# A late-tile mask moved to VectorE, transposes of one bank kept together, and a new table of offsets

## The chip, the cores and the metric

The kernel runs on one core of one Trainium2 chip. The metric is the device time of one execution in microseconds (us). Durations in the text are us unless marked ns. TensorE is called PE in the profile, VectorE DVE, ScalarE ACT, GpSimd POOL, and SyncE, which issues the loads, SP.

## What is computed

One decoder layer on 512 tokens of width 1024: token mixing, cross-attention into 256 memory tokens, and a squared-ReLU MLP of width 4096. The part that the change touches is the attention inside token mixing: 8 query heads on 2 KV heads of 64 columns, with three branches (compressed, selected, window). With 512 tokens, 8 blocks of 64 and a top-k of 16, every block is selected, so the selected branch and the window branch are both causal attention over all earlier tokens, each with its own keys and values:

```python
s = jnp.einsum('bthgd,bhtmd->bhgtm', qc, kg) * scale
p = masked_softmax(s, mask)                  # mask: key position <= query position
o_slc = einsum(p, vg)                        # the window branch is the same with its own k, v
o = g[..., 0:1] * o_cmp + g[..., 1:2] * o_slc + g[..., 2:3] * o_win
```

`masked_softmax` puts minus infinity where the mask is false, subtracts the row's maximum, takes the exponential, and divides by the sum.

## The kernel before

The Python program lists all instructions and a planner, the class `Plan`, orders them. `add` (L204) takes down each instruction with its cost (`cost`, L140), its dependences and a rank. The rank is the instruction's place in the program, moved by a lead and by an entry of the table `LEADS` (L57), which is looked up by the name of the stage. `schedule` then runs a clock per engine: `choose` (L318) takes for each engine the instructions that could start first and among these the one with the highest rank; `start` (L304) says when that would be. The order that comes out is issued as it is, the DMAs on SP's queue among it, so each engine works through a fixed list, in order. All instructions therefore show one line of the source in the profile, L405.

Matrix products are done in three passes, since each operand is split into a high and a low part (`split`: ScalarE casts the high part, VectorE subtracts it to get the low one). One PSUM bank holds 128 x 512 floats, and there are 8 of them.

Attention goes over the query tiles t = 0 to 3 of 128 rows, over the KV heads and over pairs of query heads, so there are 16 units, each with two heads (e = 0, 1), in 32 steps. A step has these parts:

- `scores` (L964): two matmuls per branch, of the query tile with the high keys `KB` and the low keys `KL`, into a bank; n = 128 (t + 1) columns. Where both branches fit into one bank (t = 0, 1) they share it. For t = 2 and 3 (n = 384 and 512) each branch b has its own bank. Then a third matmul, bf16, of the identity `idb` with `tri` (0 on and under the diagonal, -1e38 above) adds the mask to the last 128 columns.
- `soft` (L985): VectorE takes the negated row maximum from the bank (TENSOR_REDUCE), ScalarE the exponential, from the bank to an SBUF tile `P` (6 buffers), with the row sum as a second output.
- `scale`: VectorE or GpSimd multiplies `P` by the reciprocal of the sum and the gate.
- `turn`: four transposes of 128 x 128 per bank bring the `P` tiles of the unit before to the layout that the product with the values needs; in the rows they are the matmuls `ps<-idf,P`. ScalarE and VectorE split them out of the bank.
- `values` and `evac`: the products with the values, among them four with the compressed branch's `Vc` that have only 128 moving columns (`ps<-pt,Vc`).

Work that doesn't depend on attention ("fill": the gating unit, memory keys and values) is placed between these steps. After it come the output projection and the cross-attention of each row tile (the `ch_` stages; `ch_v` has further matmuls of 128 columns, `ps<-b,b`), then the two halves of the MLP, ff1 and ff2. Other fp32 transposes, with moving operand 128 x 128, are in the profile as `ps<-idf,z`, `ps<-idf,b` and `ps<-idf,bT`.

Of the kernel before, what the change touches and what calls it, by code (L numbers as in the profile page):

```python
# [9 lines left out]
F32 = mybir.dt.float32  # L10
# [43 lines left out]
         "wa": dict(w=3, raw=2),  # L54
         "wf": dict(w=1, raw=1)}

LEADS = {"ch_f0": -1174, "ch_f1": -1572, "ch_f2": -903, "ch_norm1": 1885, "ch_norm2": 867, "ch_norm3": -7928,  # L57
# [21 lines left out]


class Plan:
# [15 lines left out]

    TABLES, TABLE = {AF.Exp: 0, AF.Tanh: 0, AF.Gelu_apprx_tanh: 1}, 1283

    SPARE = (0, 300, 0, 0, 0)  # L100

    def __init__(self, tc, share):
        self.tc, self.nc, self.share = tc, tc.nc, share
        self.ops, self.loads, self.lead, self.queue, self.stage, self.stages = [], [], 0.0, None, None, []
        self.home, self.last, self.reads, self.tables = {}, {}, {}, []
        self.tiles, self.uses, self.caps, self.index = [], [], {}, {}
        for e in self.ENGINES:
            setattr(self, e, self._Engine(self, e))
# [31 lines left out]
    def cost(self, eng, op, aps, func):  # L140
        n = max(self.width(a) for a, _ in aps)
        if eng == "tensor":
            if op == "transpose" and all(a.dtype == F32 for a, _ in aps):
                return 109
            return max(25, n / 2.4 + (15 if n > 200 else 7))
        if eng == "sync":
            run = min(list(a.ap)[-1][1] for a, _ in aps)
            return max(450, 4 * n * max(list(a.ap)[0][1] for a, _ in aps) / (230 if run <= 128 else 290))
        psum = any(bank for _, bank in aps)
        part = 100 if eng != "gpsimd" and min(list(a.ap)[0][1] for a, _ in aps) < P and n > 32 else 0  # L150
        if eng == "vector" and any(len(a.ap) > 2 and list(a.ap)[-1][0] > 4 for a, _ in aps):
            part = 0.9 * n
        scalars = sum(1 for a, _ in aps if self.width(a) == 1) if n > 1 else 0
        if eng == "scalar":
            return n / 1.2 + (52 if psum else 93) + 93 * scalars + part
        if eng == "vector":
            if op == "reciprocal":
                return 68 + 6.3 * n
            fast = op in ("tensor_scalar", "tensor_copy") and not psum
            return 68 + n / (1.92 if fast else 0.96) + 61 * (scalars > (op == "tensor_reduce")) + part  # L160
        if op in ("tensor_tensor", "square"):
            return 300 + 165 * n if func == OP.pow else 150 + 2.1 * n
        return 244 + 0.84 * n + 82 * (scalars > 1) if op == "tensor_scalar" else 130 + 0.9 * n
# [40 lines left out]
    def add(self, ways, args, kw):  # L204
# [50 lines left out]
                for e, op in ways]  # L255
        self.loads.append(self.load(ways[0][1], args[1]) if ways[0][0] == 0 else 0.0)
        self.tables.append(next((self.TABLES[a] for a in args if isinstance(a, AF) and a in self.TABLES), None))
        self.stages.append(self.stage)
        self.ops.append((ways, args, kw, sorted(deps), used, self.lead + LEADS.get(self.stage, 0) - i))

    def schedule(self):
# [12 lines left out]
        active, held, uses = set(), set(), [len(u) for u in self.uses]  # L274
        ends = [{} for _ in self.tiles]
        free, begun, table = [0.0] * ne, 0.0, 0

        port = {1: 0.0, 3: 0.0}
        known = [[-1e9] * ne for _ in ops]
# [22 lines left out]
            return max([0.0] + [t + lat[x][e] for x, t in f])  # L302

        def start(i, e):  # L304
            t = max(free[e], begun + self.loads[i]) if e == 0 else free[e]
            if e == 2 and self.tables[i] not in (None, table):
                t += self.TABLE
            if e in port and next(w for w in ops[i][0] if w[0] == e)[3]:
                t = max(t, port[4 - e])
            for x in range(ne):  # L310
                t = max(t, known[i][x] + lat[x][e])
            return t
# [5 lines left out]
        def choose(e):  # L318
# [15 lines left out]
            if not ts:  # L334
                return None
            lim = min(ts)[0]
            r, t, i = max((ops[i][5], t, i) for t, i in ts if t <= lim)
            return t, -r, i, e

# [4 lines left out]
        while len(out) < len(ops):  # L344
# [25 lines left out]
                stale[4 - e] = True  # L370
            if e == 0:
                begun = t
            if e == 2 and self.tables[i] is not None:
                table = self.tables[i]
            span = max(span, end)
# [33 lines left out]
def hybrid_block(ctx, tc, x, mem, norm_mix_g, w_in, sg_ln_g, sg_ln_b, sg_w, sg_b, q_norm_g,  # L409
# [346 lines left out]
    for t in range(TT):  # L756
# [9 lines left out]
    nc.stage = "masks"  # L766
    idb = cpool.tile([P, P], BF16, name="idb")
    dve.tensor_copy(idb, idf)
    tri = cpool.tile([P, P], BF16, name="tri")
    tri32 = ztile()[:, :P]  # L770
    pool.memset(tri32, 0.0)
    pool.affine_select(out=tri32, in_=tri32, pattern=[[-1, P]], compare_op=OP.is_ge,
                       fill=NEG, base=0, channel_multiplier=1)
    dve.tensor_copy(tri, tri32)
    cmk = cpool.tile([P, TT, 32], BF16, name="cmk")
# [176 lines left out]
    class Pair:  # L952
# [11 lines left out]
        def scores(self, e):  # L964
            kvh, n = self.kvh, self.n
            g = 2 * self.pr + e
            q = self.qT[:, g * P:g * P + P]
            if 2 * n <= 512:
                S = bank()[:, :2 * n].rearrange("p (b n) -> p b n", b=2)
                for i, k in enumerate((KB, KL)):  # L970
                    nc.tensor.matmul(S, q, k[:, kvh, :, :n], start=i == 0, stop=False)
                nc.tensor.matmul(S[:, :, n - P:n], idb, bc(tri[:, None, :], [P, 2, P]), start=False, stop=True)
                self.S[e] = [S]
            else:
                self.S[e] = []
                for b in range(2):
                    S = bank()[:, :n]
                    for i, k in enumerate((KB, KL)):
                        nc.tensor.matmul(S, q, k[:, kvh, b, :n], start=i == 0, stop=False)
                    nc.tensor.matmul(S[:, n - P:n], idb, tri, start=False, stop=True)  # L980
                    self.S[e].append(S)
            self.mx[e], self.den[e] = small(2), small(2)
            self.Ps[e] = []

        def soft(self, e, b):  # L985
            Ss, mx = self.S[e], self.mx[e]
            if len(Ss) == 2:
                dve.tensor_reduce(mx[:, b:b + 1], Ss[b], AX.X, OP.max, negate=True)
            elif b == 0:
                dve.tensor_reduce(mx, Ss[0], AX.X, OP.max, negate=True)  # L990
            S = Ss[b] if len(Ss) == 2 else Ss[0][:, b, :]
            self.Ps[e].append(zpool.tile([P, 512], F32, tag="P", bufs=6, name=nm("P"))[:, :self.n])
            act(self.Ps[e][b], S, AF.Exp, bias=mx[:, b:b + 1], accum_out=self.den[e][:, b:b + 1])

        def scale(self, e):
            h = self.kvh * G + 2 * self.pr + e
# [439 lines left out]
```

## Time and profile before

| | us |
|---|---|
| median of 3 runs | 701.18 (699.33 to 701.6) |
| profiled execution, its own time | 699.56 |
| its span, first to last instruction | 697.8 |
| PE busy | 689.5 (99%) |
| DVE busy | 415.2 (59%) |
| ACT busy | 318.2 (46%) |
| POOL busy | 79.2 (11%) |
| granted TensorE clock, mean of the core | 1.000 |

How to read it: busy time of PE is modelled, since matmuls are pipelined. In a timeline the start of a matmul plus its length is its end, and the difference of two ends that follow each other is what the second one cost. Rows of several equal matmuls carry a count (x4), and their length runs from the first start to the last end.

### The profile page before, as it was taken

To read this page: it belongs to the slowest core of one execution; us is meant where nothing else is said; L and a number is where in the kernel's file an instruction comes from. 1 tells how busy PE (TensorE), PEld (TensorE's weight loads), DVE (VectorE), ACT (ScalarE), POOL (GpSimd) and SP (SyncE) were. 2 spreads that over 40 slices of the span, in tenths; PEclk is the share of its full clock that TensorE was granted. 3 is DMA by queue.
4 is the path that set the end of the run, shared out by engine and by line. 5 is a ranking of instruction groups with operands and counts; after the bars stand their busy time and mean duration, and the time that the engine had idled before them with its cause. 6 is when DMAs were issued, how large, how long until landed. Compare 5 with 4: busy or idle time off the path is not lost.

```text
span 697.8 us, 9634 instructions
## 1 busy us (share of the span) xinstructions
PE 689.5 (99%) x3632; PEld 579.0 (83%) x3632; DVE 415.2 (59%) x791; ACT 318.2 (46%) x634; POOL 79.2 (11%) x120
## 2 busy tenths in 40 slices
PE   8999999999999999999999999999999999999997
PEld 7898878888888788888988888888878888888886
DVE  6578898898999997679842432223224444334423
ACT  6544558877788774586532341424133221112210
POOL 1101103232342130133000000000000000000000
PEclk9999999999999999999999999999999999999999
DMA  9624553552223101323243333323223222232203
GB/s 284 167 86 129 156 156 119 182 189 83 62 61 91 62 1 42 111 62 92 66 116 94 88 90 98 113 74 110 91 91 115 97 91 90 97 112 93 91 0 121
DMA packets 63677, 71.03 MB, mean 102 GB/s; under 512 B 3160, under 2 KB 46928, under 8 KB 63632
## 3 DMA queue, kind: packets, MB, share of 16 engines
q1 hardware_dynamic: 63632, 70.42, 32.8%
q8 instruction: 29, 0.48, 0.3%
q14 instruction: 16, 0.13, 0.1%
HBM read 68.32 MB, written 2.10 MB: 101 GB/s over the span
## 4 chain that ended last, share of the span: by engine, by line
PE 92%; DVE 3%; ACT 3%; DMA 1%; issue 0%; SPq 0%; DVEq 0%; ACTq 0%
PE ps L405 92%; DVE b L405 1%; DVE w L405 1%; ACT w L405 1%; ACT b L405 1%; DMA raw<-in_cmp_w_dram 1%; ACT P L405 1%; DMA raw<-in_w_in_dram 1%; DVE s L405 0%; ACT KL L405 0%; DVE pc L405 0%; ACT z L405 0%; DVE P L405 0%; SPq L405 0%; DVE q L405 0%
## 5 line engine op out<-in xcount | busy, mean ns | idle before, releaser
L405 PE MATMUL ps<-w,q 128*128 128x512 f32 x960 | 225.1, 391 | 0.7 <-ACT z L405 0.7
L405 ACT CAST w<-raw 128x1024 fp32r<-128x1024 f32 (+2 forms) x96 | 98.7, 1029 | 249.5 <-PE ps L405 239.9
L405 PEld LDWEIGHTS ps<-w,q 128*128 128x128 f32 x960 | 178.5, 188 | 37.2 <-ACT z L405 1.1
L405 DVE TENSOR_TENSOR w<-raw,w 128x1024 fp32r<-128x1024 f32 (+2 forms) x113 | 133.0, 1178 | 113.0 <-ACT w L405 112.4
L405 PE MATMUL ps<-w,b 128*128 128x512 f32 (+3 forms) x832 | 188.8, 377 | 0.9 <-DVE w L405 0.7
L405 PEld LDWEIGHTS ps<-w,b 128*128 128x128 f32 (+1 forms) x832 | 142.9, 186 | 27.4 <-DVE w L405 2.7
L405 PE MATMUL ps<-b,w 128*128 128x512 f32 x720 | 164.7, 389 | 0.0
L405 PEld LDWEIGHTS ps<-b,w 128*128 128x128 f32 x720 | 134.8, 188 | 27.9
L405 DVE TENSOR_TENSOR b<-ps,b 128x512 fp32r<-128x512 f32 (+2 forms) x88 | 54.6, 636 | 9.4 <-ACT b L405 6.4
L405 PE MATMUL ps<-b,b 128*128 128x256 f32 x344 | 58.7, 293 | 0.0
L405 DVE CAST q<-b 128x512 fp32r<-128x512 f32 x27 | 11.5, 427 | 70.6 <-PE ps L405 70.5
L405 ACT CAST b<-ps 128x512 fp32r<-128x512 f32 (+1 forms) x84 | 44.0, 552 | 17.6 <-PE ps L405 16.9
L405 PEld LDWEIGHTS ps<-b,b 128*128 128x128 f32 x344 | 49.1, 192 | 1.4
L405 POOL TENSOR_SCALAR P<-P,s,gates 128x128 f32<-128x128 f32 (+3 forms) x55 | 35.4, 653 | 90.2 <-DVE s L405 76.9
L405 ACT ACTIVATE P<-ps,s 128x128 f32<-128x128 f32 (+3 forms) x64 | 33.5, 532 | 4.5 <-DVE s L405 4.3
L405 PE MATMUL ps<-idf,P 128*128 128x128 f32 x192 | 34.9, 281 | 0.0
L405 DVE TENSOR_REDUCE s<-ps 128x2 f32<-128x512 f32 (+3 forms) x56 | 32.5, 602 | 0.3 <-PE ps L405 0.2
L405 POOL TENSOR_TENSOR r<-s,negh 128x1 f32<-128x1 f32 (+2 forms) x25 | 20.2, 808 | 93.9 <-DVE s L405 93.8
L405 ACT ACTIVATE z<-ps 128x512 f32<-128x512 f32 (+3 forms) x43 | 23.0, 581 | 11.6 <-PE ps L405 11.5
L405 DVE TENSOR_TENSOR q<-b,q 128x512 fp32r<-128x512 f32 (+1 forms) x36 | 23.7, 657 | 4.6 <-ACT q L405 3.7
L405 PE MATMUL ps<-b,q 128*128 128x256 f32 (+2 forms) x96 | 26.0, 339 | 0.2 <-ACT q L405 0.2
L405 PEld LDWEIGHTS ps<-idf,P 128*128 128x128 f32 x192 | 23.5, 141 | 1.3
(154 smaller groups left out, 549.3 us busy)
## 6 DMA issues: line engine op xcount, KB each, us to landing
raw<-in_w_ff_dram SPq DMA_DIRECT2D x64, 512.0 KB, 4.0
raw<-in_w_in_dram SPq DMA_DIRECT2D x12, 512.0 KB, 4.5
raw<-in_cmp_w_dram SPq DMA_DIRECT2D x8, 512.0 KB, 4.3
raw<-in_w_out_dram SPq DMA_DIRECT2D x8, 512.0 KB, 3.8
raw<-in_w_mkv_dram SPq DMA_DIRECT2D x8, 512.0 KB, 3.8
b<-in_x_dram SPq DMA_DIRECT2D x8, 256.0 KB, 5.1
raw<-in_w_in_dram SPq DMA_DIRECT2D x8, 256.0 KB, 5.6
b<-in_x_dram SPq DMA_DIRECT2D x4, 512.0 KB, 5.7
```

The lines of the kernel that those rows point to most:

```text
L405: getattr(getattr(self.nc, eng), op)(*a, **k)
```

## The change

Four things are done.

1. In `scores`, for t = 2 and 3, the third matmul (`tri` by `idb`) goes. In `soft`, for these tiles, the reduction is replaced by VectorE's `tensor_tensor_reduce`: it reads the bank and the mask (`tri`, now 512 columns wide with zeros ahead of the triangle), writes the negated masked scores to `P` and the row minimum of these to the small tile. The exponential then reads `P` instead of the bank and writes to it in place, with scale -1. `P` is claimed by the VectorE instruction instead of by the exponential. Tiles t = 0 and 1 keep their matmul.
2. The planner keeps, for each transpose, the bank that it writes (`turns`). After a transpose, PE takes another transpose into the same bank, if one could start as early as anything else. After the first transpose of a bank, any instruction that isn't a transpose is booked 23 ns later (`ALONE`).
3. The planner books `tensor_tensor_reduce` at 76 ns plus 1/0.96 ns for an element.
4. `LEADS` gets other entries: 123 before and 101 after. 63 names stand in both, with other values. This moves ranks in all stages, loads on SP's queue included.

```diff
-LEADS = {"ch_f0": -1174, "ch_f1": -1572, ...
+LEADS = {"ch_f0": -304, "ch_norm3": -5448, ...
...
+    ALONE = 23
...
+            if op == "tensor_tensor_reduce":
+                return 76 + n / 0.96
...
+        self.turns.append(next((k for k in sorted(used) if self.tiles[k][1]), -1) if ways[0][1] == "transpose" else -1)
...
-            t = max(free[e], begun + self.loads[i]) if e == 0 else free[e]
+            t = max(free[e] + (self.ALONE if alone and self.turns[i] < 0 else 0), begun + self.loads[i]) if e == 0 else free[e]
...
             lim = min(ts)[0]
+            if e == 0 and turn >= 0:
+
+                ts = [b for b in ts if b[0] <= lim and self.turns[b[1]] == turn] or ts
...
             if e == 0:
                 begun = t
+                alone, turn = self.turns[i] >= 0 and turn < 0, self.turns[i]
...
-    tri = cpool.tile([P, P], BF16, name="tri")
-    tri32 = ztile()[:, :P]
+
+    tri = cpool.tile([P, T], BF16, name="tri")
+    tri32 = ztile()
...
                 for b in range(2):
                     S = bank()[:, :n]
                     for i, k in enumerate((KB, KL)):
-                        nc.tensor.matmul(S, q, k[:, kvh, b, :n], start=i == 0, stop=False)
-                    nc.tensor.matmul(S[:, n - P:n], idb, tri, start=False, stop=True)
+                        nc.tensor.matmul(S, q, k[:, kvh, b, :n], start=i == 0, stop=i == 1)
...
+            pt = zpool.tile([P, 512], F32, tag="P", bufs=6, name=nm("P"))[:, :self.n]
+            self.Ps[e].append(pt)
             if len(Ss) == 2:
-                dve.tensor_reduce(mx[:, b:b + 1], Ss[b], AX.X, OP.max, negate=True)
...
+                dve.tensor_tensor_reduce(out=pt, in0=Ss[b], in1=tri[:, T - self.n:], scale=-1.0, scalar=3e38,
+                                         op0=OP.add, op1=OP.min, accum_out=mx[:, b:b + 1])
+                act(pt, pt, AF.Exp, bias=mx[:, b:b + 1], scale=-1.0, accum_out=self.den[e][:, b:b + 1])
```

## Rows read from the trace of the kernel before

**Rows 1.** The page: busy time of PE, and VectorE's 40 slices in tenths.

```profile
PE 689.5 (99%) x3632; PEld 579.0 (83%) x3632; DVE 415.2 (59%) x791; ACT 318.2 (46%) x634; POOL 79.2 (11%) x120
DVE  6578898898999997679842432223224444334423
```

**Rows 2.** The page: the chain that ended last, share of the span by engine.

```profile
PE 92%; DVE 3%; ACT 3%; DMA 1%; issue 0%; SPq 0%; DVEq 0%; ACTq 0%
```

**Rows 3.** Busy time by stretch: stretch, its length, then each engine (instructions).

```profile
0.00:20.00 20.00, 17.75 (x103) 14.73 (x104) 11.38 (x21) 11.09 (x24) 3.42 (x9) 1.00 0.92 275
...
60.00:100.00 40.00, 39.18 (x214) 31.92 (x213) 34.18 (x56) 21.63 (x29) 7.81 (x11) 1.00 0.53 152
...
520.00:525.00 5.00, 4.31 (x19) 3.16 (x18) 3.11 (x4) 4.20 (x9) 0.00 (x0) 1.00 0.25 84
...
sum 690.00, PE 685.70 PEld 576.21 DVE 412.29 ACT 318.25 POOL 79.18; mean PE 45.71 PEld 38.41 DVE 27.49 ACT 21.22 POOL 5.28
```

**Rows 4.** The same view, for the late tiles' scores and the stretch after them.

```profile
181.00:258.00 77.00, 76.84 (x505) 63.72 (x504) 72.20 (x180) 60.83 (x154) 23.03 (x31) 1.00 0.18 57
258.00:340.00 82.00, 82.00 (x510) 72.02 (x509) 63.26 (x124) 51.60 (x113) 18.91 (x26) 1.00 0.21 65
```

**Rows 5.** Groups by operation and shape: busy us, mean ns of one, idle before it.

```profile
L405 DVE TENSOR_TENSOR w<-raw,w 128x1024 fp32r<-128x1024 f32 x102 | 124.7, 1224 | 109.2 <-ACT w L405 108.9
...
L405 DVE TENSOR_TENSOR b<-ps,b 128x512 fp32r<-128x512 f32 x64 | 43.0, 685 | 7.2 <-ACT b L405 6.4
...
L405 ACT ACTIVATION_READ_ACCUMULATOR P<-ps,s 128x1 f32 x64 | 13.1, 205 | 0.0
...
L405 DVE SCALAR_TENSOR_TENSOR b<-ps,r,b 128x512 f32<-128x512 f32 x16 | 11.8, 742 | 0.8 <-PE ps L405 0.6
...
L405 DVE TENSOR_REDUCE s<-ps 128x1 f32<-128x512 f32 x16 | 10.4, 676 | 0.0
...
L405 DVE TENSOR_REDUCE s<-ps 128x1 f32<-128x384 f32 x16 | 8.2, 546 | 0.1
...
L405 PE MATMUL ps<-tri,idb 128*128 128x128 bf16 x32 | 7.4, 230 | 0.0
...
L405 ACT CAST q<-ps 128x512 fp32r<-128x512 f32 x12 | 7.1, 588 | 1.8 <-PE ps L405 1.7
...
L405 ACT CAST q<-bT 128x512 fp32r<-128x512 f32 x4 | 2.5, 627 | 0.7 <-DVE bT L405 0.7
```

**Rows 6.** Timeline of PE, 236.2 to 237.6: start, length, tile, shape, count.

```profile
236.21 0.39 PE L405 MATMUL ps<-KL,q 128*128 128x512 f32 x1
236.44 0.23 PE L405 MATMUL ps<-tri,idb 128*128 128x128 bf16 x1
236.48 0.48 PE L405 MATMUL ps<-b,q 128*128 128x512 f32 x1
236.79 0.40 PE L405 MATMUL ps<-KL,q 128*128 128x512 f32 x1
237.03 0.23 PE L405 MATMUL ps<-tri,idb 128*128 128x128 bf16 x1
237.10 0.28 PE L405 MATMUL ps<-idf,P 128*128 128x128 f32 x1
237.13 0.31 PE L405 MATMUL ps<-pt,Vc 128*128 128x128 f32 x1
237.28 0.30 PE L405 MATMUL ps<-idf,P 128*128 128x128 f32 x1
```

**Rows 7.** The same view, 213.6 to 215.1.

```profile
213.67 0.64 PE L405 MATMUL ps<-b,b 128*128 128x256 f32 x4
214.15 0.22 PE L405 MATMUL ps<-pt,Vc 128*128 128x128 f32 x1
214.20 0.29 PE L405 MATMUL ps<-idf,P 128*128 128x128 f32 x1
214.25 0.53 PE L405 MATMUL ps<-pt,Vc 128*128 128x128 f32 x3
214.62 0.45 PE L405 MATMUL ps<-b,b 128*128 128x256 f32 x2
```

**Rows 8.** The same view, a run of transposes at 233.6.

```profile
233.59 0.82 PE L405 MATMUL ps<-idf,P 128*128 128x128 f32 x6
```

More of the change, by code (lines that the diff above doesn't have):

```diff
@@ L55 @@
          "wf": dict(w=1, raw=1)}
-LEADS = {"ch_f0": -1174, "ch_f1": -1572, "ch_f2": -903, "ch_norm1": 1885, "ch_norm2": 867, "ch_norm3": -7928,
[21 rows of a table removed]
+LEADS = {"ch_f0": -304, "ch_norm3": -5448, "ch_o0": 500, "ch_o0.w512.2": 3108, "ch_o1": -1711,
[17 rows of a table added]
 class Plan:
@@ L104, in __init__ @@
         self.ops, self.loads, self.lead, self.queue, self.stage, self.stages = [], [], 0.0, None, None, []
-        self.home, self.last, self.reads, self.tables = {}, {}, {}, []
+        self.home, self.last, self.reads, self.tables, self.turns = {}, {}, {}, [], []
         self.tiles, self.uses, self.caps, self.index = [], [], {}, {}
@@ L276, in schedule @@
         free, begun, table = [0.0] * ne, 0.0, 0
+        turn, alone = -1, False
         port = {1: 0.0, 3: 0.0}
@@ L768, in hybrid_block @@
     dve.tensor_copy(idb, idf)
-    tri = cpool.tile([P, P], BF16, name="tri")
-    tri32 = ztile()[:, :P]
+    tri = cpool.tile([P, T], BF16, name="tri")
+    tri32 = ztile()
     pool.memset(tri32, 0.0)
-    pool.affine_select(out=tri32, in_=tri32, pattern=[[-1, P]], compare_op=OP.is_ge,
+    pool.affine_select(out=tri32[:, T - P:], in_=tri32[:, T - P:], pattern=[[-1, P]], compare_op=OP.is_ge,
                        fill=NEG, base=0, channel_multiplier=1)
@@ L971, in scores @@
                     nc.tensor.matmul(S, q, k[:, kvh, :, :n], start=i == 0, stop=False)
-                nc.tensor.matmul(S[:, :, n - P:n], idb, bc(tri[:, None, :], [P, 2, P]), start=False, stop=True)
+                nc.tensor.matmul(S[:, :, n - P:n], idb, bc(tri[:, None, T - P:], [P, 2, P]), start=False, stop=True)
                 self.S[e] = [S]
@@ L986, in soft @@
             Ss, mx = self.S[e], self.mx[e]
+            pt = zpool.tile([P, 512], F32, tag="P", bufs=6, name=nm("P"))[:, :self.n]
+            self.Ps[e].append(pt)
             if len(Ss) == 2:
-                dve.tensor_reduce(mx[:, b:b + 1], Ss[b], AX.X, OP.max, negate=True)
[L989 to L993, printed above, removed]
+                dve.tensor_tensor_reduce(out=pt, in0=Ss[b], in1=tri[:, T - self.n:], scale=-1.0, scalar=3e38,
+                                         op0=OP.add, op1=OP.min, accum_out=mx[:, b:b + 1])
+                act(pt, pt, AF.Exp, bias=mx[:, b:b + 1], scale=-1.0, accum_out=self.den[e][:, b:b + 1])
+            else:
+                if b == 0:
+                    dve.tensor_reduce(mx, Ss[0], AX.X, OP.max, negate=True)
+                act(pt, Ss[0][:, b, :], AF.Exp, bias=mx[:, b:b + 1], accum_out=self.den[e][:, b:b + 1])
         def scale(self, e):
```

38 rows, old and new, of the table LEADS are left out of this document.

## The prediction

> **What bounds the kernel now.** I read the page's first two sections, then the chain, then the engines' busy time by stretch, then PE's timeline. PE is busy for 689.5 of 697.8 us [rows 1], and 92% of the chain that ended last is PE [rows 2], so a nanosecond of PE's work is a nanosecond of the end, unless a new wait eats it. The stretches say how much waiting there is to win: over 690 us PE is idle for 690 - 685.70 = 4.3 us. 2.25 of it lie in the first 20 us, 0.82 between 60 and 100, and 0.69 between 520 and 525 [rows 3]. Outside the first 20 us that is 2.05 us in all.
>
> The change acts in the stretch from 181 to 258 us, where the scores of the tiles t = 2 and 3 are computed. There PE is idle for 0.16 us of 77. VectorE is idle for only 77 - 72.20 = 4.8 us, and ScalarE for 16.2 [rows 4]. So in this stretch VectorE is nearly a second bound; the reader should see the slices of VectorE at 8 and 9 up to there and at 2 to 4 later [rows 1]. In the next stretch, to 340 us, VectorE has 18.7 us to spare [rows 4].
>
> **The mask matmuls that go.** There are 32 of them, 128x128 in bf16 [rows 5]. What one costs PE is read from ends. At 236.21 the low-key matmul ends at 236.60 and the mask at 236.67: 0.07 us. The next matmul, 512 columns wide, ends at 236.96, 0.29 after it, and the one behind that at 237.19, 0.23 after it: the mask costs its follower another 0.06. The second mask, at 237.03, ends at 237.26, and the transpose behind it at 237.38, 0.12 later [rows 6], against 0.11 for a transpose in a run: (0.82 - 0.27) / 5, taking 0.27 for the last one's length [rows 8]. So a transpose as follower pays 0.01. Along the timeline 19 of the 32 masks are followed by a transpose and 13 by a matmul. Sum: 32 x 0.07 + 19 x 0.01 + 13 x 0.06 = 3.2 us less work on PE. All of it lies where PE has no idle time, so I book **-3.2**. The bound from below is the masks alone, -2.2, should the followers still pay; there is no reason for more than -3.2.
>
> **The mask on VectorE.** The trace has no such instruction. The one it replaces takes 676 ns at 512 columns and 546 at 384. The nearest rows for a pass with two inputs, one of them a bank, are 685 and 742 at 512 columns [rows 5], so I take +10 to +66 ns, 32 times: 0.3 to 2.1 us more on VectorE. That is less than its 4.8 us of idle time [rows 4], and I book **0**. From below: the instruction could be faster than the reduction by some tens of ns, and that too would be hidden, since PE has no idle time to give back. From above: the row sums of the exponential show on ScalarE as an instruction of their own, 205 ns [rows 5]. With that on VectorE an instruction costs up to 742 + 205 - 676 = 271 ns more, 32 times 8.7 us, 3.9 more than the idle time. The far end is a pass at half rate, for which the subtraction over 1024 columns, 1224 ns [rows 5], is the price: (1224 - 676) x 16 + (918 - 546) x 16 = 14.7 us, with 918 as three quarters of 1224.
>
> The Trainium skill, VectorE: DVE Perf Modes, section Two Vector instructions with no wait between them, says that a vector instruction which also writes its accumulator is two instructions, the pass and a read of the accumulator. No row here shows that on VectorE, and the page has no price. By it the sum would move toward the end with 271 ns, which the row of ScalarE alone already sets.
>
> **The exponential.** It now reads SBUF: a cast of 512 columns takes 588 ns from a bank and 627 from SBUF [rows 5], so +39 ns, 32 times 1.2 us. ScalarE's 16.2 us of idle time hide it; without that cover it would be 1.2. The bank comes free when VectorE is done, an exponential earlier. This could only shorten waits of PE for banks, and there are at most 0.16 us of waits here: 0. In exchange `P` is claimed by VectorE. If no buffer is free, the wait now stands on VectorE's queue, ahead of the splits that release fill weights, and no longer on ScalarE's. The buffers turn over with two steps' delay (the unit before holds four, the present step two), so this is a cost only where the transposes of the unit before are late; I book 0 and count it with the rival on VectorE. The wider `tri` is cast once, early, between 60 and 100 us; even at the reduction's rate its 512 columns are 0.7 us [rows 5], where VectorE is idle for 5.8 us of 40 [rows 3]: 0.
>
> **Transposes kept together.** The planner books 23 ns for what follows a lone transpose. If that were a cost of breaking a run, the 179 runs in which PE now does its 390 fp32 transposes, cut to about 110 (four to a bank), would give 70 x 0.023 = -1.6 us. The rows say otherwise. Lone transposes stand beside the short matmuls with 128 columns: a `Vc` matmul ends 0.06 after the transpose before it (237.38 to 237.44), and the transpose behind it 0.14 later (237.58) [rows 6]. So the pair costs 0.20, where a transpose in a run costs 0.11 [rows 8] and a `Vc` matmul among its like (0.53 - 0.31) / 2 = 0.11 [rows 7]. The short matmul is dear without a transpose behind it, also ahead of a larger one: at 214.62 two matmuls of 256 columns take 215.07 - 214.78 = 0.29 instead of 0.24, the 0.12 each that the four at 213.67 show ((0.64 - 0.28) / 3) [rows 7]. Mixed, a pair saves 0.02 to 0.04. 66 of the 96 short matmuls now have a transpose right behind them. Kept together, four transposes go with one short matmul. I take half of the 66 as lost, at 0.03: +1.0; all of them at 0.036 would be +2.4, none 0. Fewer breaks beside large matmuls give back up to 70 x 0.01; I take -0.3. Booked: **+0.7**, with ends of -1.6 (the planner's price) and +2.4.
>
> **The new offsets.** They set every queue's order anew, the loads on SP's among them, and no row shows that order. They can't reduce PE's work, only its waits: at best 2.05 us outside the first 20 us and about half of the 2.25 in these [rows 3]. At worst they open waits; the worst later stretch of this trace has 0.82 in 40 us [rows 3], which over 181 to 340 us, now all but without waits [rows 4], would be 3.3. I book **0**, as a mean of the two ends.
>
> **Sum.** -3.2 + 0 + 0.7 + 0 = -2.5 us. Against the profiled execution (699.56, its span of 697.8 and 1.8 around it) that gives 697.1. This execution lies 1.6 under the median of the runs, so I put the forecast on the median: 701.18 - 2.5 = 698.7 us, 0.36% faster. About 0.3%, or 2.1 us, is what a measurement of this kernel can tell from no change.
>
> **Rivals.**
> - The new order closes the waits. All 2.05 us outside the first 20 us go: -4.6, 696.6 us. For it: VectorE and ScalarE are free enough after 340 us, and the waits before 100 us are for weights that SP could load in another order. Against it: before 100 us the planner has little else to give PE.
> - The new order opens waits, at the rate of the worst stretch, over 181 to 340 us: -2.5 + 3.3 = +0.8, 702.0 us. For it: there is nowhere to go but up in that stretch.
> - VectorE becomes the bound between 181 and 258 us. The mechanism is a dearer instruction on an engine with 4.8 us to spare in this stretch; the rest falls on PE, since the splits behind it feed PE's fill work. With 271 ns each: -2.5 + 3.9 = +1.4, 702.6; at half rate -2.5 + 9.9 = +7.4, 708.6. It makes the kernel slower by 0.3% from (4.8 + 2.5 + 2.1) / 32 = 0.29 us each. For it: the busy share of 94%. Against it: two-input passes run at the reduction's rate [rows 5], and the spare time after 258 us takes up a delay as long as PE has fill work.
> - The grouping doesn't do what it is booked for: at its upper end it takes back most of the masks' gain, -3.2 + 2.4 = -0.8, 700.4 us.
>
> **How the numbers follow.** I give the forecast 0.40, closed waits 0.22, opened waits 0.20, VectorE 0.10, and the grouping's loss 0.08. With a spread of 2 us the forecast is past the bound in 0.24 and within it in 0.16. Closed waits are faster (0.22). Opened waits are within in 0.10 and slower in 0.10; VectorE is slower in 0.09; the grouping's loss is within in 0.06 and faster in 0.02. With the 0.01 left of VectorE that makes 0.48 faster, 0.33 the same, 0.19 slower. The range: down to -3.2 - 1.6 - 2.05 = -6.9, 694.3 us; up past the opened waits and the first price on VectorE, with a tenth of the chance (half rate, more waits) left out: 703.5 us.
>
> **What would show it.** The profile after should have no `ps<-tri,idb` of 128x128; 32 VectorE instructions at 512 and 384 columns within 66 ns of the reductions; exponentials from SBUF some 39 ns longer; some 110 runs of transposes, and short matmuls at 0.11 where they stand together. PE's idle time outside the first 20 us should stay near 2 us. VectorE's busy time from the first to the last late score should stay under the stretch's length. The prediction is wrong if PE's idle time changes by more than 2 us, if the new instruction costs over 0.15 us more than the reduction (4.8 / 32), or if most short matmuls still find a transpose behind them.

## The result and the profile after

The changed kernel takes 696.87 us (median of 7 runs, 696.6 to 698.14), the kernel before 700.6 (7 runs). The ratio is 0.995, 95% interval 0.9938 to 0.9962: 3.5 us or 0.5% less. The forecast was 698.7 against 701.18, 0.36% less, with a range from 694.3 to 703.5. A second round beside the last experiments gave 0.995 again (0.9931 to 0.9969). The two profiled executions differ by less, 699.56 - 696.73 = 2.8 us, and so do their spans, 697.8 and 695.0. The ledger below accounts for 2.7 of this 2.8.

The page of the changed kernel (answers rows 1 and 2):

```profile
span 695.0 us, 9606 instructions
...
PE 688.1 (99%) x3600; PEld 583.3 (84%) x3600; DVE 420.8 (61%) x832; ACT 307.7 (44%) x622; POOL 80.5 (12%) x121
...
DVE  5698799988999997588832533332233444334433
...
PE 98%; DVE 1%; DMA 1%; ACT 0%; issue 0%; SPq 0%; DVEq 0%
```

PE has 32 matmuls fewer, and the chain that ended last is 98% PE where it was 92% [rows 2]. VectorE's busy time rose by 5.6 us, and it now shows 41 instructions more. 32 of these, 2.7 us, are explained below. The rest comes from the planner, which gave VectorE 28 casts of weights of 128x1024 (`w<-raw`) where it had 13, and moved some other work off it.

Busy time of the changed kernel by stretch, columns as in rows 3:

```profile
0.00:20.00 20.00, 17.95 (x100) 14.78 (x101) 12.28 (x24) 11.86 (x27) 3.42 (x9) 1.00 0.79 236
...
120.00:181.00 61.00, 59.91 (x362) 50.85 (x361) 54.22 (x137) 44.81 (x119) 17.31 (x32) 1.00 0.40 130
181.00:258.00 77.00, 77.00 (x504) 68.84 (x503) 73.27 (x216) 64.34 (x164) 23.55 (x33) 1.00 0.18 56
258.00:340.00 82.00, 82.00 (x505) 72.02 (x503) 62.51 (x123) 50.22 (x109) 13.23 (x23) 1.00 0.22 65
...
sum 690.00, PE 686.81 PEld 582.56 DVE 419.24 ACT 307.74 POOL 80.49; mean PE 114.47 PEld 97.09 DVE 69.87 ACT 51.29 POOL 13.41
```

PE is idle for 3.2 us of 690 instead of 4.3 [rows 3], and outside the first 20 us for 1.14 instead of 2.05. In the stretch of the late scores it has no idle time at all, though VectorE has only 3.7 us to spare there instead of 4.8 [rows 4].

The new instruction and its neighbours in the changed kernel, groups by shape (answers rows 5):

```profile
L412 ACT ACTIVATE P<-P,s 128x512 f32<-128x512 f32 x16 | 11.6, 727 | 1.7 <-DVE s L412 1.5
...
L412 DVE CUSTOM_DVE_ANT_0 P<-ps,tri 128x512 f32<-128x512 f32 x16 | 10.6, 684 | 0.0
...
L412 DVE CUSTOM_DVE_ANT_0 P<-ps,tri 128x384 f32<-128x384 f32 x16 | 8.4, 549 | 0.0
...
L412 DVE DVE_READ_ACCUMULATOR2_ANT s<- 128x1 f32 x32 | 2.7, 83 | 0.0
```

The pass takes 684 ns at 512 columns and 549 at 384, where the reduction took 676 and 546 [rows 5]. Behind each stands a second instruction of 83 ns that reads the accumulator. So the mask costs VectorE 91 or 86 ns an instruction, 2.8 us in all. The exponential from SBUF takes 727 ns; in the kernel before, from the bank, it took 695:

```profile
L405 ACT ACTIVATE P<-ps,s 128x512 f32<-128x512 f32 x16 | 11.0, 695 | 1.7 <-DVE s L405 1.7
```

PE's timeline in the changed kernel, about 187 us (answers rows 6 to 8):

```profile
187.06 0.84 PE L412 MATMUL ps<-b,b 128*128 128x256 f32 x5
187.74 0.56 PE L412 MATMUL ps<-pt,Vc 128*128 128x128 f32 x4
188.13 0.46 PE L412 MATMUL ps<-b,b 128*128 128x256 f32 x2
...
196.52 0.82 PE L412 MATMUL ps<-idf,P 128*128 128x128 f32 x6
```

Transposes stand in runs: six at 196.52, 0.11 each as in rows 8. The four `Vc` matmuls stand together. They end at 188.30, 0.40 after the matmuls before them (187.90), so 0.06 for the first and 0.11 for each of the others. The two wide matmuls behind them take 0.29 instead of 0.24.

**A ledger of PE's time.** Along PE's timeline, each matmul's end minus the end before it was split into the usual pitch of its kind (227 ns at 512 columns, 119 at 256, 175 at 384, 129 at 280, 109 for an fp32 transpose, 62 and 33 for a short matmul of 128 and of 64 columns, 56 for a mask of 128) and what is over. What is over goes to waits if it is large, else to the kind of neighbour it stands beside.

| us, after the first 9 us | before | after | difference | booked |
|---|---|---|---|---|
| masks, with what their followers lose | | | -3.2 | -3.2 |
| behind short matmuls (128 and 64 columns) | 5.1 | 6.8 | +1.7 | +1.0 |
| beside transposes | 1.6 | 1.7 | +0.1 | -0.3 |
| waits | 5.4 | 4.2 | -1.2 | 0 |

These sum to -2.6, with the first 9 us -2.7, against 2.8 in the spans. Fp32 transposes stand in 112 runs instead of 179, and 29 of the 96 short matmuls with 128 columns have a transpose behind them instead of 66.

### The profile page after: what moved, and what is told of

The parts are those of the page before. It is cut to its first block, busy times and chain, and to the rows that moved or that the text cites. A ratio compares the mean times of both kernels' runs of the same rounds, so it can differ in the third digit from the quotient of the medians.

```text
span 695.0 us, 9606 instructions
## 1 busy us (share of the span) xinstructions
PE 688.1 (99%) x3600; PEld 583.3 (84%) x3600; DVE 420.8 (61%) x832; ACT 307.7 (44%) x622; POOL 80.5 (12%) x121
## 4 chain that ended last, share of the span: by engine, by line
PE 98%; DVE 1%; DMA 1%; ACT 0%; issue 0%; SPq 0%; DVEq 0%
PE ps L412 98%; DMA raw<-in_w_in_dram 1%; DVE b L412 0%; DVE w L412 0%; ACT w L412 0%; SPq L412 0%; ACT z L412 0%; DVEq L1442 0%
## 5 line engine op out<-in xcount | busy, mean ns | idle before, releaser
L412 PE MATMUL ps<-w,b 128*128 128x512 f32 (+2 forms) x832 | 184.6, 375 | 0.1
L412 ACT CAST w<-raw 128x1024 fp32r<-128x1024 f32 (+2 forms) x80 | 82.2, 1029 | 206.7 <-PE ps L412 201.9
L412 PE MATMUL ps<-b,w 128*128 128x512 f32 x720 | 167.1, 390 | 0.0
L412 PE MATMUL ps<-b,b 128*128 128x256 f32 (+1 forms) x344 | 59.1, 291 | 0.0
L412 DVE CAST q<-b 128x512 fp32r<-128x512 f32 (+1 forms) x28 | 11.7, 418 | 75.8 <-PE ps L412 75.8
L412 ACT CAST b<-ps 128x512 fp32r<-128x512 f32 (+1 forms) x84 | 43.9, 548 | 20.5 <-PE ps L412 20.3
L412 DVE CAST w<-raw 128x1024 fp32r<-128x1024 f32 (+2 forms) x33 | 21.5, 652 | 51.4 <-PE ps L412 51.1
L412 POOL TENSOR_TENSOR r<-s,negh 128x1 f32<-128x1 f32 (+2 forms) x25 | 23.4, 939 | 106.2 <-DVE s L412 106.2
L412 PE MATMUL ps<-idf,P 128*128 128x128 f32 x192 | 30.9, 276 | 0.0
L412 ACT ACTIVATE P<-P,s 128x384 f32<-128x384 f32 (+1 forms) x32 | 21.6, 676 | 1.8 <-DVE s L412 1.5
```

What stands on the lines that cost most here:

```text
L412: getattr(getattr(self.nc, eng), op)(*a, **k)
```

## Experiments

All ratios are to the kernel before, with 95% intervals.

**1. The masks alone, in the order of before.** The planner makes the order as before; on issue the 32 masks are dropped, with nothing in their place (the late tiles are not masked).

```diff
+    nc.swap[len(nc.ops) - 1] = lambda: nc.nc.tensor.matmul(S, q, KL[...], start=False, stop=True)
     nc.tensor.matmul(S[:, n - P:n], idb, tri, start=False, stop=True)
+    nc.swap[len(nc.ops) - 1] = lambda: None
```

> The kernel before with its order of instructions held and the 32 mask matmuls of t = 2 and 3 left out, nothing in their place, so the late tiles are unmasked. Theory (the masks cost PE 0.07 each and their followers 0.01 or 0.06): 3.2 us less, 697.4 against 700.6, ratio 0.9954. Rival (the time goes into waits, since VectorE and ScalarE are nearly as busy from 181 to 258 us): under 1 us less, ratio above 0.9985. If followers pay without the mask too: 2.2 us less, 0.9968.

Measured: 699.1 us, ratio 0.998 (0.9966 to 0.9995), 1.4 us less (0.4 to 2.4 by the interval). That lies between the theory and its rival. The third value, 0.9968 for followers that pay without the mask too, lies just inside the interval, but the ledger speaks against it: the masks' 3.2 us are gone with what their followers lost, and waits have grown by 1.9. Nearly all of these lie between 181 and 258 us. Busy time there in this kernel, and what PE waited for from 181 to 260 us (in total, times, longest):

```profile
181.00:258.00 77.00, 76.36 (x483) 65.98 (x481) 73.29 (x181) 62.02 (x157) 23.93 (x32) 1.00 0.18 56
```

```profile
PE ps L408 <- ACT P L408: 0.2, 1, 0.2
PE ps L408 <- DVE w L408: 0.2, 1, 0.2
PE ps L408 <- ACT q L408: 0.2, 1, 0.2
```

Four pieces of its chain that ended last, in order of time (start, length, engine, tile):

```profile
220.22 1.33 DVE s L408 x3
221.55 1.13 DVE b L408 x3
223.05 0.75 DVE s L408 x2
223.80 0.96 DVE b L408 x2
```

PE is idle for 0.64 us, where it was for 0.16 [rows 4]. The page shows less than the ledger, since the modelled length of a matmul can cover a short wait. Two of PE's three waits in the list end with ScalarE, one with VectorE; between 220 and 230 the chain goes from one VectorE instruction to the next. So by the ledger more than half of the gain turned into waits for these two engines, with instruction lists on both that hadn't changed at all. That it is VectorE in the main is read from the chain; no run tests it apart from ScalarE.

**2. The masks back, in the order of the changed kernel.** On issue, each low-key matmul of a late tile is followed by the mask; VectorE adds the mask as well.

```diff
+    def masked(S=S, k=KL[:, kvh, b, :n], mask=S[:, n - P:n]):
+        nc.nc.tensor.matmul(S, q, k, start=False, stop=False)
+        nc.nc.tensor.matmul(mask, idb, tri[:, T - P:], start=False, stop=True)
+    nc.swap[len(nc.ops) - 1] = masked
```

> The changed kernel with its order held and the 32 mask matmuls put back behind the low-key matmuls; VectorE still adds the mask too. Theory: 3.2 us more than the changed kernel, about 700.1, ratio to the kernel before 0.9993. Rival (the gain came from the new order and the masks were hidden): stays at the changed kernel's 0.995.

Measured: 700.63 us, ratio 1.001 (1.0 to 1.002), 0.006 or 4.2 us more than the changed kernel's 0.995. The rival falls. The two profiled kernels have the same order on PE but for the masks, so their ends can be compared one by one: masks_back is 1.5 us behind after the first 12 us, without a mask so far, and 4.7 at the end, so the masks cost 3.2 there, and the 4.2 of the runs, some 1 either way by the intervals, fits that. In this order 22 of the masks are followed by a matmul and 10 by a transpose, so by the ledger they are worth 32 x 0.071 + 22 x 0.056 + 10 x 0.007 = 3.6 us of PE. So with the masks in place, order, grouping and new instruction together come to the kernel before; the whole gain of the change is the masks', and the new order lets PE have nearly all of it, where the old order gave 1.4 of 3.2.

**3. VectorE as the bound.** The changed kernel, order held, with an idle reduction behind each of the 32 new instructions: 256 columns, then 8.

```diff
+    nc.plus[len(nc.ops) - 1] = [lambda: nc.nc.vector.tensor_reduce(load, tri[:, :256], AX.X, OP.max)]
```

> The changed kernel with its order held and, behind each of the 32 new VectorE instructions, a reduction of 256 bf16 columns that nobody reads: about 0.41 each, 13.2 us on VectorE between 181 and 258 us, where it has 77 - 73.3 = 3.7 us to spare. The prediction's rival (what exceeds the spare time falls on PE): 13.2 - 3.7 = 9.5 us more than the changed kernel, ratio 1.0086 to before. Other theory (PE has fill work and VectorE catches up after 258 us): under 3 us more, ratio below 0.9995.

> As vector_load, with a reduction of 8 columns, about 0.15 each, 4.7 us in all, against 3.7 us to spare. If only what exceeds the spare time falls on PE: 1.0 us more than the changed kernel, ratio 0.9964. If each added VectorE microsecond falls on PE, spare time or not: 4.7 more, 1.0017.

Measured: with 256 columns 706.55 us, ratio 1.0086 (1.0073 to 1.0099), which is 9.5 us more than the changed kernel. With 8 columns 699.0 us, 0.9968 (0.9956 to 0.998); beside it the changed kernel had 0.995, so 1.3 us more. The added reductions by tile (shortest, median and longest, ns) and the late stretch, first with 256 columns:

```profile
L1006 DVE TENSOR_REDUCE load<-tri x32: 409/417/426, 186.0 to 266.2; 128x1 f32<-128x256 bf16 x32
```

```profile
181.00:258.00 77.00, 72.28 (x450) 61.88 (x448) 75.03 (x223) 59.81 (x149) 20.36 (x29) 1.00 0.18 56
```

The same with 8 columns:

```profile
L1006 DVE TENSOR_REDUCE load<-tri x32: 148/157/161, 187.7 to 260.6; 128x1 f32<-128x8 bf16 x32
```

```profile
181.00:258.00 77.00, 76.96 (x492) 67.23 (x492) 74.61 (x240) 62.02 (x157) 21.87 (x31) 1.00 0.19 63
```

32 x 0.417 = 13.3 us of work with 3.7 to spare cost 9.5, and 32 x 0.157 = 5.0 cost 1.3. Both are the work less the spare time. The 1.3 alone would be too small to tell: the two intervals overlap. The traces decide it, as PE's order is the same in both kernels. The same two instructions in the changed kernel and then with 8 columns:

```profile
199.10 0.82 PE L412 MATMUL ps<-idf,P 128*128 128x128 f32 x6
261.94 0.22 PE L412 MATMUL ps<-pt,Vc 128*128 128x128 f32 x1
```

```profile
201.13 0.82 PE L415 MATMUL ps<-idf,P 128*128 128x128 f32 x6
265.39 0.23 PE L415 MATMUL ps<-pt,Vc 128*128 128x128 f32 x1
```

The first is 2.03 us behind, lost in the first 12 us, and the second 3.45: 1.4 us were lost between, though the page shows PE idle for only 0.04 from 181 to 258. The other theory, that PE lives on fill work meanwhile, falls: PE lost 4.7 us in the late stretch of the first kernel, and the rest of the late scores moved on past 258 us. So the mechanism of the prediction's third rival and its formula were right, as far as these two loads show it. Only the price kept it from happening: 2.8 us on VectorE, under the 4.8 it had.

**4. The new table.** The changed kernel with the table of before; with an empty table; and the two planned parts alone with the table of before: the masks without the rule on transposes, and the rule without the masks. Last, the new table without the rule.

```diff
-LEADS = {"ch_f0": -304, "ch_norm3": -5448, ...
+LEADS = {"ch_f0": -1174, "ch_f1": -1572, ...        # old_offsets, masks_alone, turns_alone
+LEADS = {}                                          # no_offsets
...
-    ALONE = 23                                      # free_turns, masks_alone
+    ALONE = 0
-            if e == 0 and turn >= 0:
+            if e == 0 and turn >= 1 << 30:
```

> The changed kernel with the offsets of the kernel before: masks on VectorE and transposes kept together, planned with the old table. If the new table only moved waits by little (the forecast booked 0): within 1.5 us of the changed kernel, ratio 0.993 to 0.997. If the table is what makes the other two parts pay: at or above the kernel before, ratio 0.999 or more.

> The changed kernel without the rule that keeps transposes of a bank together and without the 23 ns; masks on VectorE and the new offsets stay, the planner orders anew. Theory (mixing transposes with short matmuls saves 0.02 to 0.04 a pair): short matmuls with a transpose behind them rise from 29 to 60 or more, PE's pitch falls by about 1 us, and the time stays within 2 us of the changed kernel, either way, as the new table was made for the rule. Rival (the planner's 23 ns is a real cost of each lone transpose): 1.6 us or more slower than the changed kernel, with PE's busy time up by that.

> The kernel before with the planner's new rule on transposes alone (masks as matmuls, old offsets). Theory: runs of transposes fall to about 112 and the short matmuls lose their partners, 0.7 us more, ratio 1.000 to 1.002 with up to 3 us of new waits on top, as the table wasn't made for it. Rival (grouping saves 23 ns a break): 1.6 us less, ratio 0.9977.

> The kernel before with the masks on VectorE alone: old rule for transposes, old offsets, the planner orders anew. Theory: 3.2 us less and 0 to 3 us of waits from an order that the table wasn't made for: ratio 0.9954 to 1.000. Rival (VectorE becomes the bound from 181 to 258 us): slower than before.

> The changed kernel with an empty table: the planner's order by program place alone. It tells how much a table is worth and how far a new one can move the time. If waits are what a table moves: PE's work by pitch is within 2 us of the changed kernel's and PE's idle time grows by what the kernel is slower, some 10 us or more (ratio 1.01).

| kernel | us | ratio | waits in the ledger | behind short matmuls |
|---|---|---|---|---|
| old_offsets | 718.29 | 1.0259 (1.0235 to 1.0283) | 25.5 | 6.6 |
| turns_alone | 717.22 | 1.024 (1.0207 to 1.0273) | 20.5 | 6.7 |
| masks_alone | 726.03 | 1.036 (1.0332 to 1.0387) | 34.7 | 5.8 |
| free_turns | 717.06 | 1.0249 (1.0219 to 1.0278) | 24.3 | 6.0 |
| no_offsets | 723.09 | 1.0323 (1.0294 to 1.0351) | 30.7 | 7.1 |

The theories for free_turns, turns_alone and masks_alone missed; in free_turns only 31 of the 96 short matmuls had a transpose behind them, where 60 were expected. For old_offsets the second of the two values came, and in no_offsets it was waits, as expected, with a ratio of 1.0323 where 1.01 was named as the least. All five go one way: a list planned with a table that wasn't made for it and its rules is 17 to 25 us slower than the kernel before. The ledger books nearly all of it as waits; its other entries stay within 2 us. Three stretches of old_offsets show it, columns as in rows 3:

```profile
120.00:181.00 61.00, 56.98 (x336) 47.88 (x334) 51.40 (x129) 41.10 (x112) 15.79 (x27) 0.97 0.39 125
181.00:258.00 77.00, 74.11 (x459) 64.55 (x457) 70.45 (x196) 56.41 (x143) 18.40 (x25) 0.98 0.21 66
258.00:340.00 82.00, 77.08 (x453) 65.90 (x452) 62.26 (x139) 49.30 (x116) 21.05 (x27) 0.98 0.20 61
```

What PE waited for in that kernel (in total, times, longest):

```profile
PE ps L416 <- DVE q L416: 3.8, 2, 2.9
PE ps L416 <- DVE b L416: 3.0, 2, 2.8
...
PE ps L416 <- DVE z L416: 1.7, 1, 1.7
```

PE's longest waits there are for steps of VectorE that come late in its list: ahead of the longest, which ends at 241.45 us, VectorE has been busy without a pause of 0.1 us since 233.5. But what the ledger books as waits is not all idle time. Outside the first 20 us PE is idle for 13.6 us in old_offsets. A part of the rest is clock: from the means of 0.97, 0.98 and 0.98 in the rows above I estimate some 10 us at 1.2 GHz, which cost PE up to 5. The timeline shows it behind a wait:

```profile
266.59 1.11 PE L416 MATMUL ps<-idf,z 128*128 128x128 f32 x4 [1.68 <-DVE z L416]
...
268.40 0.63 PE L416 MATMUL ps<-KL,q 128*128 128x512 f32 x1
268.83 0.63 PE L416 MATMUL ps<-b,q 128*128 128x512 f32 x1
```

The last two end 0.43 apart, where the usual pitch at 512 columns is 0.227. So these runs don't give what each part is worth alone; they say that in this kernel order and table are one thing. That masks_alone is the slowest doesn't show VectorE to be full: from 181 to 258 us, in which PE was busy for 67 us at a granted clock of 0.95, VectorE was busy for 64. So its rival, that VectorE becomes the bound, has the direction right, and its reason isn't shown.

```profile
181.00:258.00 77.00, 67.00 (x391) 57.37 (x390) 64.04 (x177) 51.88 (x126) 15.30 (x20) 0.95 0.16 55
```

**5. The price of a short matmul without a transpose.** In the changed kernel's order, 33 single transposes are moved to right behind a short matmul, where neither their inputs nor their bank forbid it; everything else stays. The changed kernel runs beside it.

```diff
-            for i, eng, op, _ in self.schedule():
+            for i, eng, op, _ in self.pair(self.schedule()):
```

> The changed kernel as it is, beside the two that follow: ratio 0.995 again.

> The changed kernel with its order held but for 33 single transposes, each moved to right behind a short matmul that had none there. Theory (a short matmul without a transpose behind it costs PE 0.02 to 0.04 more): short matmuls with a transpose behind them rise from 29 of 96, PE's extra time behind short matmuls falls by about 1 us, and so does the time: ratio about 0.9935. Rival (the planner's 23 ns: each lone transpose costs): 33 x 0.023 = 0.8 us slower, 0.9961. A third: banks of transposes are complete later and waits of up to 2 us open.

Measured: 697.85 us, 0.9956 (0.994 to 0.9972), against 697.61 and 0.995 (0.9931 to 0.9969) for the changed kernel: no difference that can be told, and so none by which the times alone could decide. In the ledger, the time behind short matmuls falls from 6.8 to 5.9 us, 0.027 for each transpose moved, as the theory priced it, with 55 of 96 paired instead of 29. But waits between 140 and 260 us rise by about 1 us. Nothing is left for the planner's 23 ns as the price of a lone transpose: runs rose from 112 to 144 and the time beside transposes by 0.14 us, 4 ns a run. So the price per pair is shown in the ledger. Moving these 33 transposes in this order didn't cash it: by the ledger the third theory, with waits of 1 and not 2 us, took it.

## Why the prediction came out right, point by point

- **Masks, -3.2.** Right in size on PE (experiments 1 and 2: 3.2 and 3.6 us by order). What the prediction didn't say is that the old order would have passed on only 1.4 of it. Its reason, that the stretch has no idle time on PE, was no reason for the gain to arrive: the other engines were next, and VectorE's 4.8 us of spare time didn't keep PE from waiting. That the new order would pass it on stood in no row of before; there the forecast had luck.
- **The mask on VectorE, 0.** The pass was at the near end of the bounds, +8 and +3 ns, not at +66. The rest is the read of the accumulator, an instruction of its own of 83 ns, where the prediction could only take ScalarE's 205 as its far bound. Together 2.8 us, outside the 0.3 to 2.1 that was booked as likely and inside the spare time, as was needed. The limit named, 0.15 us an instruction, was right: at 0.088 nothing was lost, and with another 0.157 there was a loss of what lay over the spare time (experiment 3). The wait for a free `P` on VectorE's queue didn't show: the new instruction has 0.0 us of idle time before it. One reading of the prediction was wrong, that VectorE's slices fall to 2 to 4 behind the late scores: from 262 to 349 us they are at 6 to 9 [rows 1]. Nothing in the sum hung on it. That a vector instruction which also writes out its accumulator is two instructions, the pass and the read, is the rule of the Trainium skill (VectorE: DVE Perf Modes, section Two Vector instructions with no wait between them). The trace agrees: 32 reads behind 32 passes.
- **The exponential.** Booked at +39 ns, measured 727 against 695 at 512 columns, +32, hidden on ScalarE.
- **Transposes kept together, +0.7.** The sign was right and the size too small: +1.8 in the ledger. Of the 66 pairs 37 were lost, as taken (half), and cost 1.2 us. The step that failed is the count of short matmuls: the 44 of 64 columns (32 `ps<-KC,q` and 12 `ps<-q,z`), which also stood beside transposes (23 of them, now 7), were left out and cost 0.5. And fewer breaks gave nothing back, where 0.3 was booked.
- **The new offsets, 0.** Waits outside the first 20 us fell from 2.05 to 1.14 by the page's idle time and by 1.2 in the ledger, a part of the second forecast case's 2.05. The reasoning was the weakest step: bounds of -3 and +3.3 around an unknown order hold only for an order that was made for these instructions. Five plans in which table and list weren't made for each other lay 17 to 25 us higher (experiment 4). That the new one lies where the old one did could not be read from the trace of before.
- **Sum.** -3.2 + 0 + 0.7 + 0 = -2.5 was booked, -3.2 + 0 + 1.8 - 1.2 = -2.6 is what the ledger has: two terms missed by about 1 us, in opposite directions. That the sum came out is luck to that extent. The medians lie 3.7 apart, 0.9 more than the two profiled executions. Of before, that execution is 1.0 below its median, of the changed kernel 0.1; the prediction added its sum to the median and so expected no more than the 2.5.

What stays open: what keeping transposes together is worth in an order made without it. Free_turns can't say, as its table was made for the rule.

## What to carry to other kernels

Work taken off the bounding engine is worth its length only if the engine that is next finds its steps in time: give that engine's spare time in the same stretch beside the gain, and treat added work there as free up to it and at full price beyond, as two added loads came out here. That it is spare in sum doesn't say that it lies where it is needed, as experiment 1 shows. The table of offsets of this planner belonged to one list of instructions and rules; where a kernel has such a table, test a part of such a change with the order held, since re-planning with the wrong table cost 17 us and more here, where the parts are worth 1 to 4. Count all small matmuls beside an instruction whose order is to change, also those that the changed code doesn't name.

## What the runs showed of the hardware

A short matmul of 128 columns costs PE 0.08 with a transpose behind it, 0.06 for itself and 0.02 that the transpose loses, and 0.11 without, and by the ledger 33 transposes moved there gave back 0.027 each.

Profiled executions of kernels with the same start differ there by up to 2 us. The runs of experiment 5's kernel lie at 697.2 to 697.9 and at 699.2; only the one that was profiled, at 699.16, shows why. That execution, and that of the changed kernel, from 6 to 10 us:

```profile
6.00:10.00 4.00, 3.27 (x11) 2.41 (x12) 3.10 (x6) 2.40 (x4) 0.00 (x0) 0.70 1.05 330
```

```profile
6.00:10.00 4.00, 3.53 (x16) 2.73 (x17) 3.74 (x6) 2.54 (x5) 0.00 (x0) 1.00 1.05 324
```

In the first, a load of the tokens kept PE waiting for 1.74 us at 6.73, and the granted clock then is 0.70 in the mean of these 4 us, part of them at 1.2 GHz. In the second the wait was 0.91 and the clock stayed at 2.4. The timelines give the price, first that kernel's and then the changed one's:

```profile
6.73 0.65 PE L479 MATMUL ps<-idf,b 128*128 128x128 f32 x4 [1.74 <-DMA b<-in_x_dram]
7.15 3.31 PE L479 MATMUL ps<-w,b 128*128 128x512 f32 x7
```

```profile
6.40 0.66 PE L412 MATMUL ps<-idf,b 128*128 128x128 f32 x4 [0.91 <-DMA b<-in_x_dram]
6.81 3.38 PE L412 MATMUL ps<-w,b 128*128 128x512 f32 x12
```

Seven matmuls of 512 columns instead of twelve in the same time, some 1.4 us at 0.28 each. With 8 columns (experiment 3) the start looks the same, with a wait of 1.64 us and a granted clock of 0.79 from 6 to 10 us. So differences under 2 us between two profiled executions of this kernel have to be looked for at its start first.
